# A planned encoder block on one core: paired reciprocals, a narrower port model, one more kind of wait, and new due times

## The chip, the cores and the metric

The kernel runs on one core of one Trainium2 chip. That core has a matrix engine (TensorE; PE in the profile, its weight loads PEld), a vector engine (VectorE; DVE), a scalar engine (ScalarE; ACT), a general engine (GpSimd; POOL) and a sync engine (SyncE; SP) that here only issues DMAs. Each engine takes its instructions in order; between engines, semaphores order them. The metric is the time of one execution on the device in microseconds (us); less is better. Three runs of the kernel before took 702.26, 703.32 and 703.99 us, median 703.32.

## What is computed

One encoder layer on 512 tokens of 1024 features, float32. In short (shapes, masks and gains left out where they don't matter here):

```python
hn = rms_norm(h, ln_mix)
z = hn @ w_in                      # 3590 columns, for three groups of heads
# A: 4 heads, two softmaxes each:  a = probs(q1, k1) - lam * probs(q2, k2);  o = a @ v; rms_norm(o)
# B: 6 heads, one softmax, bias from the cumulative log forget gate, causal
# C: 6 heads, one softmax, bias from a table of clipped relative positions
h = h + concat(o_a, o_b, o_c) @ w_out
u = rms_norm(h, ln_ffn) @ w_up     # 2 x 2816 columns
c = causal depthwise convolution of width 3 over u
h = h + (silu(gate) * val) @ w_down
h = h + (p @ w_ple_proj) * sigmoid(rms_norm(h, ln_ple) @ w_ple_gate)
```

Every query and key head is RMS-normed over its 64 features before the products. A softmax is `exp(s - max)` divided by its row sum; the division is a reciprocal of one number per row, and a multiplication of the row by it. For A, `probs(q1, k1)` and `probs(q2, k2)` have a reciprocal each, and the second is multiplied by `-lam` as well.

## The kernel before

**Products.** Matrices are float32, split into a high part of a shorter type (fp32r) and the rest: `split` casts a weight tile (`wraw`) to `whi` on ScalarE and subtracts on VectorE or GpSimd to get `wlo`. `mm3` then makes three products (high with high, high with low, low with high) into one bank of PSUM. There are eight banks, under the tags `z` (2), `s` (2), `t` (3) and `o` (1).

**Two stages, two plans.** The first stage (projections, attention, the output projection) and the second (the MLP, its down projection, the gate with the per-layer embedding) are each recorded as a list of operations before anything is issued. An object of class `Plan` then puts the list in order. All instructions are issued by one helper (`Engine.now`), so nearly all rows of the profile have line L363, and tiles tell them apart.

**How a plan makes an order.** `price` gives each operation a duration (`busy`) and a lag from its form and width. `due` gives each TensorE operation a due time: the sum of TensorE durations before it, plus a shift by the name of its group from the table `SHIFT`; every other operation is due ahead of the operations that need it. `solve` steps through time, and gives each engine that is free the ready operation that is due first, with a few rules for waiting a moment for a more urgent one. The order that comes out is the program order of all engines, and of the DMAs on SP's and POOL's queues. `SHIFT` has some 330 numbers between -30 and 30 us, of which no formula is given.

**The port in the plan.** `price` sets `op.port` for every GpSimd operation that is no DMA, and for VectorE's `tensor_scalar`, `tensor_tensor` and `scalar_tensor_tensor` whose inputs all lie outside PSUM. In `solve`, an operation with `port` of one of the two engines isn't begun while one of the other is under way. This is a matter of the plan; on the chip nothing enforces it but the order itself. There is one exception, in `emit`: in the second plan (where `late` is 0.1; in the first it is 0) a GpSimd operation of over `LONG` = 0.6 us by its price, whose predecessor among the operations with `port` is a VectorE operation, gets a true wait on that operation (`behind`).

**Attention.** `scores(pr, hh, qbs)` runs over blocks of 128 queries (`qb` 0 to 3) of head `hh` of a pair `pr`; the block `qb` has (qb + 1) x 128 keys. `softmax_map` makes the scores (two products into `s`), a combined add-bias and row minimum on VectorE into `e` and `st`, the exponential on ScalarE with its row sum into `st[:, 1:2]`, and the reciprocal on VectorE into `st[:, 2:3]`. Then GpSimd multiplies `e` by it (group B and C), or, for A, multiplies the second map's `e2` by its reciprocal and `-lam`, and VectorE joins both maps. `prob_cols` transposes the `e` of all four blocks of a head, and `values` makes the products with V into the bank `o`; the result goes to `oall` over `otmp`. `subln` norms the heads of A.

**The narrow GpSimd work.** `qk_sums` makes the norms of queries and keys: a square on ScalarE, a sum on VectorE, then for each token block a multiply and a power on GpSimd, 128x4 (`rs`); `qk_scale` on VectorE uses it to evacuate the bank into `zn`. `token_stats` does the like with one column (`rstd`). Between them GpSimd has the wide work: moves of halves of `q` and `k` (64x512), the scaling of `e`, some of the `wlo` subtractions of the first stage (`lo_by` chooses which, 128x768 and 128x512), sums and differences of weights in the second, and DMAs that add into a weight tile.

The price of the two kinds of GpSimd operation that matter for the wait: a subtraction of n columns is 0.1 + 0.0024 n us, a power of four columns 0.42 + 4 x 0.155, both times 1.05.

Of the kernel before, what the change touches and what calls it, by code (L numbers as in the profile page):

```python
# [8 lines left out]
F32 = mybir.dt.float32  # L9
# [3 lines left out]
ALU = mybir.AluOpType  # L13
# [28 lines left out]
for _i in range(3):  # L42
# [2105 lines left out]
```

## Time and profile before

| | us |
|---|---|
| median of three runs | 703.32 |
| the profiled execution | 702.13 |
| its span (first to last instruction) | 700.4 |
| TensorE busy | 686.6 |
| VectorE busy | 574.8 |
| ScalarE busy | 425.9 |
| GpSimd busy | 315.2 |

The span lies within the time of the execution. The granted TensorE clock is 1.0 for all of it. Busy times of different engines lie beside each other and don't add up to the span; a TensorE that is busy nearly all the time leaves other engines' idle time without a price of its own.

A row of the timeline has the start and the length in us, the engine, the line, the operation, what it writes and reads, its shapes and, in brackets, how long the engine was idle before it and what ended that. A row of waits has the engine and tile that waited, what it waited for, then us in total, how many times, and the longest.

### The profile page before, as it was taken

To read this page: it belongs to the slowest core of one execution; us is meant where nothing else is said; L and a number is where in the kernel's file an instruction comes from. 1 tells how busy PE (TensorE), PEld (TensorE's weight loads), DVE (VectorE), ACT (ScalarE), POOL (GpSimd) and SP (SyncE) were. 2 spreads that over 40 slices of the span, in tenths; PEclk is the share of its full clock that TensorE was granted. 3 is DMA by queue.
4 is the path that set the end of the run, shared out by engine and by line. 5 is a ranking of instruction groups with operands and counts; after the bars stand their busy time and mean duration, and the time that the engine had idled before them with its cause. 6 is when DMAs were issued, how large, how long until landed. Compare 5 with 4: busy or idle time off the path is not lost.

```text
span 700.4 us, 12856 instructions
## 1 busy us (share of the span) xinstructions
PE 686.6 (98%) x4600; PEld 642.4 (92%) x4600; DVE 574.8 (82%) x1159; ACT 425.9 (61%) x810; POOL 315.2 (45%) x418
## 2 busy tenths in 40 slices
PE   7999999999999999999999999999999999999997
PEld 7989999998899888899899899888999888999997
DVE  6788888888778766898989987889888889867777
ACT  6756776666557664766667644557445665436853
POOL 3686776757657544242332243232442312343650
PEclk9999999999999999999999999999999999999999
DMA  9533624333221152595875246774368663223433
GB/s 324 217 99 91 171 58 134 92 95 101 76 76 47 60 121 86 186 270 127 209 180 163 84 140 156 175 193 129 89 153 225 171 168 107 86 73 88 143 102 122
DMA packets 42989, 94.32 MB, mean 135 GB/s; under 512 B 4870, under 2 KB 9606, under 8 KB 42924
## 3 DMA queue, kind: packets, MB, share of 16 engines
q1 hardware_dynamic: 35868, 79.02, 35.8%
q0 software_dynamic: 6768, 14.16, 11.9%
q8 instruction: 36, 0.59, 0.3%
q10 hardware_dynamic: 288, 0.30, 0.1%
q14 instruction: 29, 0.24, 0.1%
HBM read 85.20 MB, written 4.21 MB: 128 GB/s over the span
## 4 chain that ended last, share of the span: by engine, by line
PE 89%; POOL 3%; DMA 3%; DVE 2%; issue 1%; ACT 1%; POOLq 0%; ACTq 0%; DVEq 0%
PE z L363 41%; PE s L363 21%; PE t L363 19%; PE o L363 8%; DMA wraw<-in_w_up_dram 2%; POOL k L363 2%; POOL q L363 1%; DMA zn<-in_w_in_dram 0%; POOL wraw L363 0%; DVE conv L363 0%; POOL wlo_again L363 0%; ACT whi L363 0%; DVE wlo L363 0%; ACT otmp L363 0%; DVE xl_again L363 0%
## 5 line engine op out<-in xcount | busy, mean ns | idle before, releaser
L363 ACT CAST whi<-wraw 128x768 fp32r<-128x768 f32 (+2 forms) x146 | 109.4, 762 | 51.9 <-PE z L363 16.5
L363 DVE TENSOR_TENSOR wlo<-wraw,whi 128x768 fp32r<-128x768 f32 (+2 forms) x128 | 113.8, 901 | 17.3 <-ACT whi L363 16.3
L363 PE MATMUL z<-whi,Th 128*128 128x384 f32 (+2 forms) x360 | 123.1, 348 | 4.6 <-ACT whi L363 4.6
L363 PE MATMUL z<-whi,Tl 128*128 128x384 f32 (+2 forms) x360 | 122.9, 347 | 0.1
L363 PE MATMUL z<-wlo,Th 128*128 128x384 f32 (+2 forms) x360 | 122.5, 346 | 0.0
L363 PEld LDWEIGHTS z<-whi,Th 128*128 128x128 f32 x360 | 67.9, 189 | 7.9 <-ACT whi L363 4.6
L363 PEld LDWEIGHTS z<-whi,Tl 128*128 128x128 f32 x360 | 67.8, 189 | 3.8 <-DVE Tl L363 0.5
L363 PEld LDWEIGHTS z<-wlo,Th 128*128 128x128 f32 x360 | 67.8, 189 | 3.2
L363 POOL TENSOR_TENSOR wraw<-wraw,wraw 128x768 f32<-128x768 f32 (+2 forms) x21 | 29.7, 1416 | 66.9 <-DVE pin L363 25.9
L363 ACT ACTIVATE e<-e,st 128x128 f32<-128x128 f32 (+3 forms) x80 | 44.7, 560 | 23.7 <-DVE st L363 23.0
L363 PE MATMUL s<-Tl,whi 128*128 128x512 f32 (+1 forms) x152 | 51.9, 341 | 0.0
L363 PE MATMUL s<-Th,whi 128*128 128x256 f32 (+1 forms) x152 | 51.7, 342 | 0.0
L363 PE MATMUL s<-Th,wlo 128*128 128x256 f32 (+1 forms) x152 | 51.7, 341 | 0.0
L363 PE MATMUL z<-Th,wlo 128*128 128x256 f32 (+1 forms) x152 | 51.4, 340 | 0.0
L363 PE MATMUL z<-Tl,whi 128*128 128x256 f32 (+1 forms) x152 | 51.3, 340 | 0.0
L363 PE MATMUL z<-Th,whi 128*128 128x256 f32 (+1 forms) x152 | 51.2, 341 | 0.0
L363 POOL TENSOR_TENSOR rs<-rs,nhalf 128x4 f32<-128x4 f32 x40 | 42.3, 1060 | 5.4 <-DVE rs L363 2.9
L363 DVE CUSTOM_DVE_ANT_0 e<-s,bias 128x128 f32<-128x128 f32 (+3 forms) x74 | 34.0, 471 | 11.7 <-PE s L363 9.1
L363 POOL TENSOR_SCALAR e<-e,st 128x512 f32<-128x512 f32 (+3 forms) x48 | 28.4, 602 | 24.4 <-DVE st L363 19.4
L363 PE MATMUL t<-wlo,ah 128*128 128x256 f32 x116 | 32.7, 282 | 0.0
L363 PE MATMUL t<-whi,al 128*128 128x256 f32 x116 | 32.7, 282 | 0.0
L363 PE MATMUL t<-whi,ah 128*128 128x256 f32 x116 | 32.4, 282 | 0.0
(341 smaller groups left out, 2281.2 us busy)
## 6 DMA issues: line engine op xcount, KB each, us to landing
wraw<-in_w_up_dram SPq DMA_DIRECT2D x41, 384.0 KB, 4.6
wraw<-in_w_in_dram SPq DMA_DIRECT2D x28, 384.0 KB, 3.9
wraw<-in_w_down_dram SPq DMA_DIRECT2D x17, 384.0 KB, 3.1
wlo_again<-in_w_up_dram SPq DMA_DIRECT2D x12, 384.0 KB, 3.7
whi_again<-in_w_up_dram SPq DMA_DIRECT2D x11, 384.0 KB, 3.9
wraw<-in_w_out_dram SPq DMA_DIRECT2D x16, 256.0 KB, 2.8
wraw<-in_w_up_dram SPq DMA_DIRECT2D x16, 256.0 KB, 4.1
wlo<-wraw POOLq DMA_DIRECT2D x7, 384.0 KB, 4.5
```

The source lines that it names most:

```text
L363: ins = getattr(self.eng, op)(*a, **k)
```

## The change

Four things are changed.

1. `softmax_map` no longer takes the reciprocal. `scores` gives two maps one tile `st` of 2 x 4 columns (six of them in turn, where there were twelve of 4), and takes both reciprocals in one VectorE instruction once both maps have their row sums. For A the two maps are those of one block; for B and C they are those of the blocks 0 and 1, and 2 and 3, and both scalings on GpSimd come after the second one's exponential.
2. In `price`, only an operation with an operand of at least 64 columns has `port`. So `rs`, `rstd` and other small GpSimd operations, and small VectorE ones, no longer hold the port or wait for it in the plan.
3. In `emit`, the wait of a GpSimd operation for the VectorE operation with `port` ahead of it is made in the first plan too, for operations of over 1.2 us by their price.
4. All numbers of `SHIFT` are new.

```diff
 SHIFT = {
-    "in1_1": 0.6, "in1_2": -16.6, "A0a": 11.4, "in1_3": 2.9, "in2_0": 13.5, "in2_1": 16, "A0b": 24, "in2_2": 0.5,
...
+    "in1_1": -30, "in1_2": -25.3, "A0a": -24.2, "in1_3": -30, "in2_0": -16, "in2_1": -7.6, "A0b": 0.1, "in2_2": 0.8,
...
 }
...
         here = [v for v in op.ins if v.tensor.space != bass.MemoryType.PSUM]
-        op.port = e == "pool" and not op.move or e == "dve" and (
-            len(here) == len(op.ins) and (op.name == "tensor_scalar" or op.name in ("tensor_tensor", "scalar_tensor_tensor")))
+        wide = max(self.width(v) for v in op.outs + op.ins) >= 64
+        op.port = wide and (e == "pool" and not op.move or e == "dve" and (
+            len(here) == len(op.ins) and op.name in ("tensor_scalar", "tensor_tensor", "scalar_tensor_tensor")))
...
             if op.port:
-                if before and op.eng.name == "pool" and before.eng.name == "dve" and op.busy > self.LONG and self.late:
+                if before and op.eng.name == "pool" and before.eng.name == "dve" and op.busy > (self.LONG if self.late else 1.2):
                     op.eng.behind(op.ins, before.ins)
                 before = op
...
-    def softmax_map(m, hh, qb, bias, rowb, name):
+    def softmax_map(m, hh, qb, bias, rowb, st, name):
...
-        st = ap.tile([P, 4], F32, tag="st", bufs=12, name=f"{name}_st")
...
         act.activation(e, e, AF.Exp, scale=-1.0, bias=init, accum_out=st[:, 1:2])
-        dve.reciprocal(st[:, 2:3], st[:, 1:2])
-        return e, st
+        return e
...
-        for qb in qbs:
+        maps = 2 if kind == "A" else 1
+        for n, qb in enumerate(qbs):
             bq = BIAS[pr, hh](qb)
             rowb = fq[:, qb, hd : hd + 1] if kind == "B" else None
-            e, st = softmax_map(QK[pr, 0], hh, qb, bq, rowb, f"{pr}_{hh}_{qb}")
-            if kind == "A":
-                yield
-                e2, st2 = softmax_map(QK[pr, 1], hh, qb, bq, rowb, f"{pr}_{hh}_{qb}b")
-                pool.tensor_scalar(e2, e2, st2[:, 2:3], X["nlam"], ALU.mult, ALU.mult)
-                dve.scalar_tensor_tensor(e, e, st[:, 2:3], e2, ALU.mult, ALU.add)
-            else:
-                pool.tensor_scalar(e, e, st[:, 2:3], 1.0, ALU.mult, ALU.mult)
-            PROB[pr, hh].append(e)
+            if maps == 2 or n % 2 == 0:
+                st = ap.tile([P, 2, 4], F32, tag="st", bufs=6, name=f"{pr}_{hh}_{qb}_st")
+                es = []
+            for m in range(maps):
+                es.append(softmax_map(QK[pr, m], hh, qb, bq, rowb, st[:, len(es)], f"{pr}_{hh}_{qb}_{m}"))
+                if m + 1 < maps:
+                    yield
+            if len(es) == 2:
+                dve.reciprocal(st[:, :, 2], st[:, :, 1])
+                e, e2 = es
+                if maps == 2:
+                    pool.tensor_scalar(e2, e2, st[:, 1, 2:3], X["nlam"], ALU.mult, ALU.mult)
+                    dve.scalar_tensor_tensor(e, e, st[:, 0, 2:3], e2, ALU.mult, ALU.add)
+                    es = [e]
+                else:
+                    for j in range(2):
+                        pool.tensor_scalar(es[j], es[j], st[:, j, 2:3], 1.0, ALU.mult, ALU.mult)
+                PROB[pr, hh] += es
```

87 rows, old and new, of the table SHIFT are left out of this document.

## The prediction, made before the result was known

> **What bounds the kernel now.** I read the head of the page first, then a table of two stretches, then who makes TensorE's weight loads wait, then the timeline around the longest waits.
>
> ```profile
> span 700.4 us, 12856 instructions
> ...
> PE 686.6 (98%) x4600; PEld 642.4 (92%) x4600; DVE 574.8 (82%) x1159; ACT 425.9 (61%) x810; POOL 315.2 (45%) x418
> ...
> PE 89%; POOL 3%; DMA 3%; DVE 2%; issue 1%; ACT 1%; POOLq 0%; ACTq 0%; DVEq 0%
> ```
>
> TensorE is busy 686.6 us of a span of 700.4, and the chain that ended last runs through it for 89%. What can be won is its idle time, so the next view splits that by the two plans of the kernel. Columns: stretch, length, then busy time and count for PE, PEld, DVE, ACT and POOL, the granted clock, DMA share, GB/s.
>
> ```profile
> 4.60:297.00 292.40, 288.04 (x1729) 268.27 (x1730) 231.68 (x646) 191.27 (x443) 177.58 (x275) 1.00 0.40 119
> 297.00:695.90 398.90, 398.50 (x2872) 374.09 (x2871) 340.77 (x508) 232.35 (x365) 133.98 (x133) 1.00 0.54 146
> ```
>
> The clock is 1.00 in both. The first plan (attention; its end at about 297 us is my reading) has 292.40 - 288.04 = 4.36 us of TensorE idle after the first product, the second (the MLP and the gate) 398.90 - 398.50 = 0.40. Before the first product and after the last lies what no order of the middle can win:
>
> ```profile
> 4.60 1.01 PE L363 MATMUL z<-whi,Th 128*128 128x384 f32 x2 [4.60 <-ACT whi L363]
> ```
>
> ```profile
> 695.65 0.28 PE L363 MATMUL z<-whi,al 128*128 128x256 f32 x1
> ...
> 697.39 0.33 SPq L363 DMA_DIRECT2D out_dram<-xl_again  x1
> ```
>
> The start costs 4.60 us (a load and a cast come first); from the last matmul to the end of the span run 700.4 - 695.65 = 4.75. Busy time on TensorE hides part of a stall, because a matmul's end lies well behind the start of the next one. The weight loads show the stalls from the other side (engine, tile, what it waited for: us, times, longest):
>
> ```profile
> PEld s L363 <- POOL k L363: 3.6, 4, 1.3
> PEld s L363 <- DVE st L363: 1.6, 3, 0.7
> PEld o L363 <- ACT otmp L363: 1.3, 1, 1.3
> PEld z L363 <- issue: 1.0, 4, 0.2
> PEld z L363 <- DVE conv L363: 0.9, 2, 0.6
> ```
>
> Without "issue", which waits for nothing that an order could change, the four named groups are 3.6 + 1.6 + 1.3 + 0.9 = 7.4 us. The two readings, 4.36 + 0.40 = 4.76 and 7.4, bound what is to be won from both sides; I take the middle, 6.1, that is 0.82 of each weight-load figure. So the whole change plays for under 0.9% of 703.3 us, and nothing in it makes a matmul shorter.
>
> **Where the waits come from.** The wait on `otmp` has its cause five us earlier:
>
> ```profile
> 156.79 1.87 POOL L363 TENSOR_TENSOR wlo<-wraw,whi 128x768 fp32r<-128x768 f32 x1 [0.23 <-ACT whi L363]
> ...
> 156.86 2.61 DVE L363 TENSOR_TENSOR wlo<-wraw,whi 128x768 fp32r<-128x768 f32 x1
> ```
>
> ```profile
> 160.56 0.69 DVE L363 TENSOR_TENSOR oall<-o,otmp 64x512 f32<-64x512 f32 x1
> ...
> 160.81 1.04 POOL L363 TENSOR_TENSOR rs<-rs,nhalf 128x4 f32<-128x4 f32 x1
> ...
> 161.29 0.63 ACT L363 ACTIVATE otmp<-oall 128x512 f32<-128x512 f32 x1 [1.30 <-DVE oall L363]
> 161.36 0.94 DVE L363 TENSOR_TENSOR wlo<-wraw,whi 128x768 fp32r<-128x768 f32 x1
> ...
> 161.97 0.30 PEld L363 LDWEIGHTS o<-otmp,oall 128*128 128x128 f32 x2 [1.26 <-ACT otmp L363]
> ```
>
> A long POOL subtraction starts 0.07 us ahead of a VectorE subtraction with two SBUF inputs, and the latter takes 2.61 us; the same form takes 0.94 us in the second fence. VectorE is late by 2.61 - 0.94 = 1.67 us, `oall` comes late, then `otmp`, and TensorE's load waits 1.26. The second fence shows a thing more: the `wlo` of 161.36 starts while a narrow POOL power (160.81, 1.04 us) is under way and isn't held up at all. The waits on `k` are the opposite collision:
>
> ```profile
> 176.23 0.95 DVE L363 TENSOR_TENSOR wlo<-wraw,whi 128x768 fp32r<-128x768 f32 x1
> 176.23 1.42 POOL L363 TENSOR_SCALAR k<-k 64x512 fp32r<-64x512 f32 x1
> ...
> 177.70 0.30 PEld L363 LDWEIGHTS s<-k,q 128*128 128x128 f32 x2 [1.33 <-POOL k L363]
> ```
>
> Both start at 176.23, VectorE goes first, and the POOL copy takes 1.42 us. All copies of that kind:
>
> ```profile
> L363 POOL TENSOR_SCALAR k<-k x30: 613/618/2027, 38.9 to 258.2; 64x512 fp32r<-64x512 f32 x30
> ```
>
> **The change, part by part.**
>
> *Reciprocals two at a time.*
>
> ```profile
> L363 DVE RECIPROCAL st<-st x80: 140/158/167, 43.9 to 268.0; 128x1 f32<-128x1 f32 x80
> ...
> L363 DVE SCALAR_TENSOR_TENSOR st<-st,fq x24: 200/214/683, 127.7 to 193.4; 128x1 f32<-128x1 f32 x24
> ```
>
> 40 of the 80 go: 40 x 0.158 = 6.3 us less on VectorE in the first plan (a two-element one costs what a one-element one does, since fixed cost is nearly all of 0.158 us; bounds for the saving 0 to 6.3). VectorE is busy 231.68 of 292.40 us there, so it has slack, and TensorE's weight loads wait for `st` only 1.6 us in all. I cost it through that term below. For the groups B and C the pair costs something: the first block's scaling waits for the second block's exponential, and then stands ahead of the second's on POOL.
>
> ```profile
> L363 POOL TENSOR_TENSOR rs<-rs,nhalf 128x4 f32<-128x4 f32 x40 | 42.3, 1060 | 5.4 <-DVE rs L363 2.9 <-DVE fa L363 0.2
> L363 POOL TENSOR_SCALAR k<-k 64x512 fp32r<-64x512 f32 x30 | 23.7, 792 | 5.6 <-ACT e L363 2.2 <-ACT k L363 2.1
> ...
> L363 POOL TENSOR_SCALAR rs<-rs,rstd 128x4 f32<-128x4 f32 x32 | 11.8, 368 | 22.9 <-DVE rs L363 21.5
> ...
> L363 POOL TENSOR_SCALAR e<-e,st 128x384 f32<-128x384 f32 x12 | 7.9, 664 | 1.6 <-DVE st L363 1.3 <-PE z L363 0.2
> ...
> L363 POOL TENSOR_TENSOR wlo<-wraw,whi 128x768 fp32r<-128x768 f32 x3 | 5.6, 1854 | 0.6 <-ACT whi L363 0.5
> ...
> L363 POOL TENSOR_TENSOR wlo<-wraw,whi 128x512 fp32r<-128x512 f32 x3 | 3.8, 1286 | 4.8 <-ACT whi L363 4.8
> ```
>
> (Columns: out<-in, shapes, count, busy us and mean ns, idle before.) The last pair of a head pays one 384-wide scaling, 0.664 us, between the last exponential and the last scaling. It is hidden by the projections that TensorE has queued beside the attention: in the list of its waits above no group on `e` reaches the 0.9 us of the last one shown. I take 0. Uncovered in all 12 heads it would be 12 x 0.664 = 8.0 us; I give that no more than the tail beyond the range. The four heads of A lose nothing, as their two maps were already joined at the second scaling.
>
> *Long POOL operations wait in the first plan too.* The rows above show which are over 1.2 us there: three subtractions of 768 (1.854 us) and three of 512 (1.286 us); the powers, at 1.060, and the copies of `k`, at 0.792, stay below. At most six waits are added. Behind a waiting one stand on POOL the next `rs`, `k` or `e`, late by at most one VectorE subtraction (0.94 us). What goes is the case of 156.8: I take the whole of its TensorE wait, 0.82 x 1.3 = -1.1 us (bounds 0 and -1.3).
>
> *Narrow operations no longer hold the port in the plan.* No instruction changes by this; the planner's clock does. Half of it fits the trace, by the `wlo` at 161.36: VectorE was planned around powers (40 of 1.060 us) that don't hold it. The other half does not:
>
> ```profile
> 106.16 0.68 DVE L363 SCALAR_TENSOR_TENSOR fbias<-otmp,fbias 128x512 f32<-128x512 f32 x1
> ...
> 106.34 1.42 POOL L363 TENSOR_SCALAR rs<-rs,rstd 128x4 f32<-128x4 f32 x1
> ...
> 106.75 0.95 DVE L363 TENSOR_TENSOR wlo<-wraw,whi 128x768 fp32r<-128x768 f32 x1
> ```
>
> A four-element POOL multiply, 0.262 us at its least, takes 1.42 us here and ends after two VectorE operations with two SBUF inputs. The new plan believes that it needn't wait. The Trainium skill, SBUF — State Buffer, section "Who interferes with whom", says that a VectorE instruction with two SBUF inputs contends with any GpSimd instruction that reads SBUF, and names no width; by that rule the narrow exemption would be wrong both ways. The trace agrees for POOL (1.42 us) and disagrees for VectorE (0.94 us beside a power). Going by the page alone, VectorE would gain nothing either, and the 2.2 us that I take below for `k` and `st` would be missing: about 703.2. What this does to the time is the second rival below.
>
> ```profile
> L363 POOL TENSOR_TENSOR rs<-rs,nhalf x40: 1006/1018/1487, 28.6 to 225.4; 128x4 f32<-128x4 f32 x40
> ...
> L363 POOL TENSOR_SCALAR rs<-rs,rstd x32: 262/267/1421, 44.2 to 224.9; 128x4 f32<-128x4 f32 x32
> ```
>
> Of the 32 multiplies more than half run at 0.267 or less; their excess is 11.8 - 32 x 0.262 = 3.4 us, and that of the powers 42.3 - 40 x 1.006 = 2.1. If a plan that no longer heeds them adds a third to these 5.5 us, POOL is 1.8 us later in all. How much of that TensorE feels I take from the `k` copies: 30 x (0.792 - 0.613) = 5.4 us of excess stand beside 3.6 x 0.82 = 3.0 us lost, 0.55. So +1.0 us (bounds: -0.6 if a third of the excess goes instead, +3.0 if it doubles). The narrow VectorE sum `st<-st,fq` (0.214 us, 0.683 at most) loses its place in the same way; its 24 cases are in that bound.
>
> *Due times chosen anew.* Every engine's order is drawn afresh, both plans, the loads on SP's queue and the POOL-issued ones among them. The `k` and `st` waits are missed appointments of an order that was meant to have none; a new order keeps some and makes others. Between 0 and all of them gone (bounds -0.82 x 5.2 = -4.3 and, if as many come as there were, +4.3) I take half of what there is, because VectorE's planned times now lie nearer to the measured ones: `k` -0.82 x 3.6 / 2 = -1.5, `st` -0.82 x 1.6 / 2 = -0.7. For the second plan I take 0, as it loses only 0.40 us.
>
> **Sum:** -1.1 + 1.0 - 1.5 - 0.7 = -2.3 us, to be held against the profiled execution: 702.13 us, its span of 700.4 and 1.7 around it, so a span of 698.1 and 699.8 us. The three runs shown have a median of 703.32, 1.2 above the profiled one; against it the forecast is **701.0 us**.
>
> **The rivals.**
>
> 1. *The waits move, and don't shrink:* half of the old ones go and as many come. For it: every order is new, and the collisions of `k` with `wlo` are between wide operations, which both plans treat alike. Against it: the measured case of 156.8. Time 703.3.
> 2. *Slower: narrow POOL work comes late.* The `rs` chain frees the projections' banks and opens the transposes. If its excess doubles, +5.5 x 0.55 = +3.0, and no other wait goes: 706.3. It decides from 2.1 / 0.55 = 3.8 us of added POOL excess on. For it: the 1.42 us row. Against it: `rs` is in none of the waits of TensorE shown, so a bank's slack takes some first.
> 3. *Slower: a load in the second plan comes too late for its split.*
>
> ```profile
> wraw<-in_w_up_dram SPq DMA_DIRECT2D x41, 384.0 KB, 4.6
> ```
>
> One such load exposed whole is 4.6 us; on top of rival 1 that gives 707.9. Against it: 0.40 us of idle in 398.90 means loads run well ahead.
> 4. *It doesn't do what it says:* the added wait is made only where a VectorE operation on the port stands directly ahead in the plan. If none of the six is so placed, and the collision comes again, 1.1 us of the sum are missing: 702.1.
>
> **How the numbers follow.** 0.3% of 703.3 is 2.1 us, about what a measurement of this kernel tells from no change, so faster means under 701.2 and slower over 705.4. Forecast 0.48 (own range 697.2, which is all 6.1 us won, to 701.2); rival 1 0.25; rival 4 0.10; rival 2 0.12; rival 3 0.05. Faster 0.48, same 0.25 + 0.10 = 0.35, slower 0.17. For the range I leave about 0.08 out below and 0.10 above: 697.5 lies just inside the ceiling, 706.5 just beyond rival 2 and short of rival 3.
>
> **What would show it.** Right: 40 reciprocals of two elements; no VectorE subtraction of 768 near 2.6 us in the first 297 us; weight-load waits for `k` near 1.8 us and for `otmp` gone; idle of TensorE after the first product near 2.5 us in the first plan and still under 1 in the second. The mean of the narrow `rs` multiplies should rise a little above 0.368 us. Wrong: new groups of waits of over 1 us on `rs`, `zn` or `e` (the pairing or the narrow ones cost what I hid), or loads and splits ahead of TensorE in the second plan; a start or an end that differs by more than 0.5 us would be a part that I held fixed.

## The result, and the profile after

The changed kernel takes 697.02 us (median of four runs, 696.18 to 697.96) against 703.41 for the kernel before (four runs): ratio 0.9912, 95% interval 0.9894 to 0.9929. That is 6.4 us less, where 2.3 were forecast, and 0.5 us below the low end of the range. The profiled execution took 696.18 us, 5.95 less than the profiled one of before.

The head of the page after, with the chain of waits (shares of the span by engine):

```profile
span 694.4 us, 12836 instructions
...
PE 684.5 (99%) x4600; PEld 642.3 (92%) x4600; DVE 570.7 (82%) x1119; ACT 424.9 (61%) x810; POOL 311.3 (45%) x418
...
PE 97%; POOL 1%; DMA 0%; DVE 0%; ACT 0%; issue 0%; POOLq 0%; ACTq 0%
```

The same two stretches as before, the second now up to the last matmul; the columns are stretch, length, then busy time and count for PE, PEld, DVE, ACT and POOL, clock, DMA share, GB/s:

```profile
4.60:297.00 292.40, 291.57 (x1753) 272.29 (x1754) 230.82 (x611) 193.99 (x450) 174.88 (x278) 1.00 0.42 123
297.00:689.90 392.90, 392.90 (x2848) 369.99 (x2846) 337.51 (x502) 228.64 (x358) 132.78 (x131) 1.00 0.54 145
```

TensorE's idle time after the first product falls from 4.36 to 292.40 - 291.57 = 0.83 us in the first stretch and from 0.40 to nothing in the second. Busy time hides part of a stall, so the matmuls themselves say more. By 297 us 1753 of them have begun, 24 more than before. Just before the end of the first stage there is a point where both kernels have made the same 1713 products, by tiles and shapes. The next matmul stands here first for the changed kernel and then for the one before; the third row is the last matmul of the changed kernel:

```profile
288.67 0.39 PE L365 MATMUL z<-whi,Th 128*128 128x512 f32 x1
```

```profile
293.83 0.39 PE L363 MATMUL z<-wlo,ah 128*128 128x512 f32 x1
```

```profile
689.67 0.28 PE L365 MATMUL z<-whi,al 128*128 128x256 f32 x1
```

At the first point the changed kernel is 293.83 - 288.67 = 5.2 us ahead. The last matmul starts 695.65 - 689.67 = 5.98 us earlier, so about 5 us are won in the first stage and about 1 us in the second; 694.4 - 689.67 = 4.7 us remain behind it, as before. The start is unchanged too. The whole gain lies in waits between, and the weight loads name them (engine, tile, what they waited for: us, times, longest):

```profile
PEld z L365 <- ACT whi L365: 4.6, 1, 4.6
PEld s L365 <- POOL k L365: 1.2, 4, 0.5
PEld z L365 <- ACT sq L365: 1.0, 1, 1.0
PEld t L365 <- DVE ptl L365: 0.4, 1, 0.4
```

The first row is the start. `k` has gone from 3.6 to 1.2 us. The six rows that are left out make 1.5 us, of 0.4 and less each; VectorE's `st` (1.6 before) and `conv` (0.9) and ScalarE's `otmp` (1.3) are in none of them. GpSimd's groups (out<-in, shapes, count, busy us and mean ns, idle before) and the new reciprocal:

```profile
L365 POOL TENSOR_TENSOR rs<-rs,nhalf 128x4 f32<-128x4 f32 x40 | 42.6, 1068 | 5.7 <-DVE rs L365 3.2
L365 POOL TENSOR_SCALAR k<-k 64x512 fp32r<-64x512 f32 x30 | 18.9, 630 | 1.9 <-ACT k L365 0.4
L365 POOL TENSOR_SCALAR rs<-rs,rstd 128x4 f32<-128x4 f32 x32 | 13.7, 427 | 18.9 <-DVE rs L365 16.4 <-DVE st L365 0.5 <-DVE V L365 0.4
...
L365 DVE RECIPROCAL st<-st 128x2 f32<-128x2 f32 x40 | 6.5, 162 | 2.6 <-ACT e L365 2.5
```

The wide copies of `k` hardly meet VectorE's wide work any more: seven of them took over 0.9 us before and one does now (0.93 us at 201.18), and their mean falls from 792 to 630 ns, near their undisturbed 613. The narrow `rs` multiplies go the other way, from 368 to 427 ns. The timeline (start, length, engine, operation; in brackets the idle time before and what ended it) has the one place where TensorE feels that:

```profile
222.34 0.69 DVE L365 TENSOR_TENSOR Tl<-oall,Th 128x512 fp32r<-128x512 f32 x1
...
222.40 1.50 POOL L365 TENSOR_TENSOR rs<-rs,nhalf 128x4 f32<-128x4 f32 x1
...
223.93 0.48 DVE L365 SCALAR_TENSOR_TENSOR zn<-z,rstd,rs 128x256 f32<-128x256 f32 x1 [0.91 <-POOL rs L365]
...
224.56 0.47 PE L365 MATMUL z<-whi,Th 128*128 128x512 f32 x1 [0.66 <-DVE zn L365]
```

A power, 1.006 us at its least before, takes 1.50 beside a VectorE operation with two SBUF inputs; `zn` waits 0.91 us for it and TensorE 0.66 for `zn`. The multiply just ahead, at 221.49, took 0.82 us in place of 0.262. The 1.0 us on `sq` among the weight loads is this same stall.

### The profile page after: what moved, and what is told of

The parts are those of the page before. It is cut to its first block, busy times and chain, and to the rows that moved or that the text cites. A ratio compares the mean times of both kernels' runs of the same rounds, so it can differ in the third digit from the quotient of the medians.

```text
span 694.4 us, 12836 instructions
## 1 busy us (share of the span) xinstructions
PE 684.5 (99%) x4600; PEld 642.3 (92%) x4600; DVE 570.7 (82%) x1119; ACT 424.9 (61%) x810; POOL 311.3 (45%) x418
## 3 DMA queue, kind: packets, MB, share of 16 engines
q0 software_dynamic: 6768, 14.16, 11.8%
## 4 chain that ended last, share of the span: by engine, by line
PE 97%; POOL 1%; DMA 0%; DVE 0%; ACT 0%; issue 0%; POOLq 0%; ACTq 0%
PE z L365 46%; PE s L365 23%; PE t L365 20%; PE o L365 8%; POOL rs L365 1%; DMA zn<-in_w_in_dram 0%; POOL q L365 0%; POOL k L365 0%; DVE zn L365 0%; DVE xl_again L365 0%; ACT q L365 0%; ACT whi L365 0%; ACT xl_again L365 0%; DVE ptl L365 0%; DVE rs L365 0%
## 5 line engine op out<-in xcount | busy, mean ns | idle before, releaser
L365 PE MATMUL s<-Th,whi 128*128 128x512 f32 (+1 forms) x152 | 51.3, 341 | 0.0
L365 PE MATMUL z<-Th,wlo 128*128 128x512 f32 (+1 forms) x152 | 51.2, 341 | 0.0
L365 POOL TENSOR_TENSOR rs<-rs,nhalf 128x4 f32<-128x4 f32 x40 | 42.6, 1068 | 5.7 <-DVE rs L365 3.2
L365 POOL DMA_DIRECT2D wraw<-in_w_up_dram x21 | 18.3, 883 | 38.4 <-DMA wraw<-in_w_up_dram 26.1
L365 POOL TENSOR_SCALAR e<-e,st 128x256 f32<-128x256 f32 (+3 forms) x48 | 26.6, 566 | 17.2 <-DVE st L365 16.6
```

What stands on the lines that cost most here:

```text
L365: ins = getattr(self.eng, op)(*a, **k)
```

## The experiments

Each ratio is against the kernel before on the same chip (medians of 702.2 to 703.1 us), with its 95% interval; times in us of different groups of runs come from different chips, so the ratios compare better. "Idle" is TensorE's idle time between 4.6 and 297 us.

### One part at a time, with the order held

These four keep every engine's order, as orders come from the plan and the edits are made at the issue of an instruction. First the changed kernel without the added wait:

```diff
-                if before and op.eng.name == "pool" and before.eng.name == "dve" and op.busy > (self.LONG if self.late else 1.2):
+                if before and op.eng.name == "pool" and before.eng.name == "dve" and op.busy > self.LONG and self.late:
```

> The changed kernel in the same order on every engine, without the three waits that the first plan's rule adds (two subtractions of 128x768 on POOL, one of 128x512). If the wait carries the gain (my step: -1.1 us): the POOL subtraction and a VectorE one with two SBUF inputs collide again, VectorE is late by up to 1.7 us, and the time goes from 697.0 to about 698. If the new order carries it: 697.0, within 0.5.

Measured: 698.59 us, ratio 0.9942 (0.9925 to 0.9958). The timelines of the place, in the changed kernel and then without the wait:

```profile
180.97 0.96 DVE L365 TENSOR_TENSOR wlo<-wraw,whi 128x768 fp32r<-128x768 f32 x1
...
182.16 1.84 POOL L365 TENSOR_TENSOR wlo<-wraw,whi 128x768 fp32r<-128x768 f32 x1 [1.22 <-PE t L365]
```

```profile
180.59 1.84 POOL L365 TENSOR_TENSOR wlo<-wraw,whi 128x768 fp32r<-128x768 f32 x1
180.66 2.58 DVE L365 TENSOR_TENSOR wlo<-wraw,whi 128x768 fp32r<-128x768 f32 x1
...
184.03 0.33 PE L365 MATMUL t<-ident,zn 128*128 128x128 f32 x1 [0.92 <-DVE ptl L365]
```

The collision of before comes back (2.58 us in place of 0.96), and TensorE stands 0.92 us. Idle goes from 0.83 to 1.76. As the order is the same, each matmul can be held against its own: 0.97 us are lost at this place and 1.2 us near 356 us, in the second stage, where nothing was changed. There a load comes late. The same GpSimd sum there, in the changed kernel and then without the wait:

```profile
352.26 0.74 POOL L365 TENSOR_TENSOR wraw<-wraw 128x256 f32<-128x256 f32 x1 [2.32 <-DVE wlo L365]
```

```profile
354.69 0.74 POOL L365 TENSOR_TENSOR wraw<-wraw 128x256 f32<-128x256 f32 x1 [3.52 <-DMA wraw<-in_w_up_dram]
```

It waits for VectorE in the one and for a DMA in the other. The load before that one, also issued by GpSimd, took 9.45 us to land in place of 8.25; GpSimd waited for it, and issued the next at 349.19 us in place of 347.83. The next two runs of the changed order have this late load and a stall behind it near 356 us too, whatever their edit, so it isn't laid to the wait. In all three the first stage ends 0.8 to 1.5 us later than in the changed kernel; whether the load is late because of that stays open. Of the changed kernel one execution has a trace, its fastest of four.

Second, the changed kernel with 80 reciprocals of one element in the places of the 40:

```diff
+            if op.name == "reciprocal" and len(op.a[0].ap) > 1 and op.a[0].ap[1][1] == 2:
+                for j in range(2):
+                    op.ins = op.eng.now(op.name, [real(v)[:, j : j + 1] for v in op.a], {})
+                continue
```

> The changed kernel in the same order, but each two-element reciprocal is issued as two of one element, one behind the other: 80 again, 40 x 0.16 = 6.3 us more on VectorE in the first plan. If VectorE's load there is what TensorE waited for: 1 to 3 us slower than 697.0. If it is slack (my reading was that it counts only by the waits on st): under 0.7 us.

Measured: 697.99 us, ratio 0.9939 (0.9922 to 0.9955), idle 292.40 - 291.47 = 0.93 us. That is 1.0 us over the changed kernel's 697.02, and more by the ratios, so by the time alone it is no case of slack. The trace puts most of the loss elsewhere. VectorE is busy 232.65 us in the first stretch, only 1.8 more, and TensorE's idle is 0.1 us longer. Matmul by matmul the run is 0.24 us late at 8.6 us, ahead of the first reciprocal (58.3 us), and 0.76 at 182 us. The other 2.4 us of its 3.2 arise near 356 and 453 us, where the first stage's reciprocals are long past. Fewer reciprocals as such bring at most 0.5 us.

Third, both undone at once, so that only the new order remains:

> The changed kernel with its order on every engine, but with the reciprocals one at a time and without the added waits, so that only the new order is left of the change. Theory A (the order carries the gain; the wait is worth 1.1 to 1.6 us as in the run without it, the pairing nothing): 698.3 to 699.5 us, ratio 0.994 to 0.997 (0.9942 was measured without the waits), TensorE idle of 1.5 to 2.5 us between 4.6 and 297 us. Theory C (the pairing and the wait help only together, and undoing both costs more than the sum): 700.5 us or more.

Measured: 698.76 us against 702.63, ratio 0.9943 (0.9928 to 0.9958), idle 1.85. The order alone is worth 0.57% (0.42 to 0.72), 4.0 us of the 6.2 that 0.9912 makes. Matmul by matmul against the changed kernel, 1.1 us are lost at the place of the wait and 1.65 near 356 us, of 3.2 in all. So the order may be worth more than 4.0 us, if the late load isn't its own.

Fourth, the reverse: the kernel before with nothing but the wait, so the first diff the other way round. Three of its six long subtractions get it.

> The kernel before with its order on every engine and one edit, the added wait of GpSimd operations of over 1.2 us in the first plan; three of six subtractions get it. Theory A (the collision at 156.8 us goes, as the prediction's step had it): 1.1 us less than the kernel before, ratio 0.9984, no VectorE subtraction of 768 columns near 2.6 us there, and no wait on otmp. Rival 4 of the prediction (the wait is not on the VectorE operation that collides): no change, ratio 1.000, the subtraction stays at 2.6 us.

Measured: 702.37 us against 702.63, ratio 1.0002 (0.9985 to 1.0019). That holds the 1.000 of rival 4, and theory A's 0.9984 lies just outside. The trace decides what the times can't:

```profile
157.95 0.95 DVE L363 TENSOR_TENSOR wlo<-wraw,whi 128x768 fp32r<-128x768 f32 x1
...
159.04 1.85 POOL L363 TENSOR_TENSOR wlo<-wraw,whi 128x768 fp32r<-128x768 f32 x1 [1.39 <-ACT ptc L363]
```

```profile
4.60:297.00 292.40, 288.98 (x1730) 269.40 (x1731) 230.31 (x646) 191.37 (x444) 177.85 (x275) 1.00 0.40 119
```

The subtraction that took 2.61 us takes 0.95, GpSimd's now stands behind it, `otmp` holds up no load, and idle falls from 4.36 to 3.42. Matmul by matmul this run is 1.04 us late at 10.1 us, ahead of anything that the edit touches, and level again at the load of `otmp` (161.94 us against 161.97), so about 1.1 us are won at that place. The mechanism is as predicted; that the time of an execution falls by it isn't shown.

### Due times exchanged, and taken away

The changed kernel with the table of before, and the kernel before with the new table:

```diff
 SHIFT = {
-    "in1_1": -30, "in1_2": -25.3, "A0a": -24.2, "in1_3": -30, "in2_0": -16, "in2_1": -7.6, "A0b": 0.1, "in2_2": 0.8,
+    "in1_1": 0.6, "in1_2": -16.6, "A0a": 11.4, "in1_3": 2.9, "in2_0": 13.5, "in2_1": 16, "A0b": 24, "in2_2": 0.5,
...
```

> The changed kernel with the due times of before: paired reciprocals, the new port rule and the added wait, in an order of their own. Theory A (the plan's clock now fits the chip, whatever the due times): most of the gain stays, about 698 to 699.5. Theory B (the gain lies in due times chosen for this plan): 702 to 706, with stalls of TensorE of 6 to 12 us after the first product.

> The kernel before with the new due times alone. Theory A: about as before, 702 to 704, since the plan still misjudges narrow operations. Theory B: the due times fit another plan, so 703 or more, up to 710. A third theory, that the due times are better by themselves: under 699.

Measured: 735.21 us, ratio 1.0464 (1.0445 to 1.0483), and 732.44 us, 1.0421 (1.0396 to 1.0445). Idle is 18.0 and 19.4 us, and both times lie far above what either theory gave. The granted clock, 1.00 in the two kernels, falls to 0.95 and 0.93 in single stretches of 50 us, so part of the loss should be slower matmuls. These two tables are worth something only with the plan for which they were made; under the other rule each is worse than none, as the next four show. They have no table at all (`SHIFT = {}`): the changed kernel; the kernel before; the changed kernel with the old port rule (`wide = True`); and the changed kernel with one reciprocal for each map, taken at once and used as before. All but the kernel before have the added wait.

```diff
         act.activation(e, e, AF.Exp, scale=-1.0, bias=init, accum_out=st[:, 1:2])
+        dve.reciprocal(st[:, 2:3], st[:, 1:2])
         return e
...
-            if len(es) == 2:
-                dve.reciprocal(st[:, :, 2], st[:, :, 1])
+            if maps == 2:
```

> The changed kernel with an empty table of shifts, so that every due time is the plain sum of TensorE's work before it. Theory A (the three parts of the change make a plan that the chip can keep, and due times only polish it): 700 to 710, far under the 735 of due times that were chosen for another plan. Theory B (all lies in the choice of due times): 725 to 740, like the two runs with borrowed due times.

> The kernel before with an empty table of shifts. Theory A: at least 6 us slower than the changed kernel with an empty table, most of it in the first 300 us. Theory B: the same as that one within 3 us.

> The changed kernel with an empty table and the port rule of before, in which narrow operations hold the port in the plan; paired reciprocals and the added wait stay. If the port rule is the part that counts: within 3 us of the kernel before with an empty table. If pairing and wait count: within 3 us of the changed kernel with an empty table.

> The changed kernel with an empty table and one reciprocal for each map, taken and used as before; the new port rule and the added wait stay. If the port rule is the part that counts: within 2 us of the changed kernel with an empty table. If the pairing counts: slower by 3 to 8 us, about VectorE's 40 x 0.16 = 6.4 us.

| without a table | us | ratio (95%) | idle, us |
|---|---|---|---|
| old rule, single (before) | 719.71 | 1.0245 (1.0219 to 1.0271) | 7.61 |
| old rule, paired | 715.64 | 1.0209 (1.0154 to 1.0263) | 5.87 |
| new rule, paired (after) | 712.20 | 1.0150 (1.0099 to 1.0202) | 5.48 |
| new rule, single | 708.22 | 1.0078 (1.0057 to 1.0099) | 1.56 |

The new rule, with the wait, takes 11.5 us off the single kernel; that is clear of noise. The steps between neighbours in the table are not, as their intervals overlap or touch: the new rule takes 3.4 us off the paired kernel, and pairing takes 4.1 off under the old rule (with the wait) and adds 4.0 under the new one. With the order held, pairing was worth at most 0.5 us; so such 4 us, if they are real, are those of another order, which any edit to the list may draw. The changed kernel without a table is 2 us above the 710 of theory A and far under theory B; the kernel before is 7.5 us slower still, as theory A had it. Of the last two runs neither came out as one of its two expectations had it, least of all the single kernel, which is 4 us faster where 3 to 8 slower or no change was expected.

### Due times searched for each rule

If a table belongs to its plan, each rule should be judged with tables of its own. For each kernel here a table was searched by random changes, kept where the plan ended earlier by its own prices, somewhat varied; no time of the chip went into it. Two tables were made for three of the rules, the second with a somewhat shorter search. How far each search went isn't shown here. The third rule is the one that the rows above suggest for narrow operations: they wait in the plan for a wide one of the other engine, but hold up none.

```diff
-        wide = max(self.width(v) for v in op.outs + op.ins) >= 64
-        op.port = wide and (e == "pool" and not op.move or e == "dve" and (
+        op.wide = max(self.width(v) for v in op.outs + op.ins) >= 64
+        op.port = (e == "pool" and not op.move or e == "dve" and (
...
-            if op.port:
+            if op.port and op.wide:
                 held[e] = t0 + busy
```

> The changed kernel with one edit, the port rule of before (narrow operations hold the port in the plan), and due times searched for this plan. The three kernels sent with it got a search of the same length. It answers whether the gain belongs to the port rule or to a lucky table. Theory A (the port rule: with narrow operations on the port some waits of TensorE on k, st or oall can't be planned away): 700 to 704 us, TensorE idle of 2 to 5 us between 4.6 and 297 us, copies of k with a mean of 0.70 us or more. Theory B (the luck of a table; any rule does as well when its due times are searched): within 1.5 us of the kernel with due times searched under the new rule, idle under 1.5 us.

> The changed kernel without the pairing (a reciprocal for each map, each map scaled at once), with the new port rule and the new wait, and due times searched for this plan. Theory A (the port rule and due times made for it carry the gain, pairing nothing): 696 to 699 us, idle of TensorE under 1.5 us between 4.6 and 297 us. Theory C (pairing is needed, since it takes 6 us off VectorE): 700 us or more, with waits on st or zn of over 1 us.

> The changed kernel with all its code, and a table of due times searched afresh in the same way as for the other kernels sent here. It is the control: it tells how far two tables made for one plan differ. Theory A: 696 to 699 us, idle of TensorE under 1.5 us between 4.6 and 297 us, as in the changed kernel. Theory B (the changed kernel's table is a lucky one): 700 us or more.

> The changed kernel with the port rule that the traces show: a narrow GpSimd operation waits in the plan for a wide VectorE one with two SBUF inputs, but holds up none itself; due times searched for this plan. Theory A with this asymmetry: narrow rs multiplies fall back from a mean of 0.427 us to 0.35 us or less, the one wait on rs at 222 us goes, 695.5 to 697.5 us. If the narrow delay costs TensorE nothing anyway (it was felt once, for 0.7 us): within 1 us of the kernel with due times searched under the new rule, with the shorter rs multiplies all the same.

The old rule came out as its theory A had it in time and idle (702.52 us, 2.14 us), though its `k` copies did not (0.674 us). The single kernel, at 703.18 us, is where theory C had it, with loads waiting 2.5 us on `st`; but pairing isn't what it lacks, since the paired control came out worst, 707.14 us. That is ten above the changed kernel with the same code, as theory B had it: the changed kernel's table is a lucky one, or a better searched one. The third rule's 698.08 us lies 0.6 above its expectation, and not by the way given: its `rs` multiplies average 0.455 us, not under 0.35, and one wait on `rs` (1.0 us) remains. In the control's trace stands why it is slow, in part:

```profile
130.16 2.15 POOL L363 TENSOR_TENSOR wlo<-wraw,whi 128x768 fp32r<-128x768 f32 x1
130.21 0.08 DVE L363 DVE_READ_ACCUMULATOR2_ANT st<- 128x1 f32 x1
130.33 2.01 DVE L363 SCALAR_TENSOR_TENSOR st<-st,fq 128x1 f32<-128x1 f32 x1
...
132.99 0.50 PE L363 MATMUL s<-k,q 128*128 128x512 f32 x1 [1.21 <-DVE st L363]
```

The narrow sum `st<-st,fq`, 128 x 1 with two SBUF inputs, takes 2.01 us beside a wide GpSimd subtraction, where 0.21 is usual. The new rule says that it needs no port. What follows it on VectorE is late, and TensorE stands 1.21 us for it. The next run tests this: the same order, with three subtractions issued behind the sums that they met, and made to wait for them.

```diff
+        for p in [q for q in order if q.port and q.eng.name == "pool" and q.busy > 1.2 and not self.late]:
+            met = [q for q in order if q.narrow and p.start - q.busy < q.start < p.start + p.busy]
...
+                    order.insert(order.index(met[-1]) + 1, p)
...
+                op.eng.behind(op.ins, last[id(op)].ins)
```

> The run with due times searched afresh (707.14 us), with the same order on every engine, but three GpSimd subtractions of 768 columns of the first plan wait for the narrow VectorE sum st<-st,fq that they met in it. In that run two of these sums took 2.01 and 1.38 us beside a subtraction, and TensorE stood 1.37 us at 131.4 right after the first. Theory D (the new rule forgets that a narrow VectorE operation is held up by a wide GpSimd one, and a table that lets them meet pays for it): the sums fall to 0.3 us or less there, the waits on st fall by 1.2 to 2.5 us, and the time to 704.5 to 706.0 us. Theory B (these meetings are hidden, or the waiting GpSimd work is late in its turn): 706.5 to 708 us.

Measured: 704.45 us, 2.7 less, ratio 1.0024 (1.0014 to 1.0033); the two traces lie 2.2 us apart.

```profile
130.43 0.22 DVE L373 SCALAR_TENSOR_TENSOR st<-st,fq 128x1 f32<-128x1 f32 x1
130.57 0.28 DVE L373 CUSTOM_DVE_ANT_0 e<-s,bias 128x128 f32<-128x128 f32 x1
130.74 1.84 POOL L373 TENSOR_TENSOR wlo<-wraw,whi 128x768 fp32r<-128x768 f32 x1 [0.20 <-DVE st L373]
```

The sum is back at 0.22 us, and the subtraction is only 0.6 us later. So the harm of the narrow VectorE exemption is shown, at 2 to 3 of the 10 us; TensorE's stalls that are left behind the start are of 1.1 us at most, and no run here takes them apart. Then a second table for each rule:

> The changed kernel with the port rule of before and a second table of due times, searched for that plan. Theory A (the rule sets what a table can reach): 700 to 705 us, near the first table's 702.5. Theory B (luck of the table): 5 us or more from the first table of the same rule, in either direction.

> The changed kernel with a second searched table. Theory D (the new rule leaves narrow VectorE sums to meet wide GpSimd work, so that tables for it scatter by what they happen to meet): anywhere from 697 to 708 us, with a mean of the 24 sums st<-st,fq that goes with the time (0.268 us in the changed kernel, 0.382 in the first searched table). Theory A (the new rule alone makes good tables, and the first searched one was a bad draw): 696 to 699 us.

> The rule by which narrow operations of both engines wait in the plan for wide ones but hold up none, with a second searched table. Theory D (this rule is the one that the chip follows, so its tables come out near each other): 697 to 700 us, the sums st<-st,fq at a mean under 0.3 us. Theory B (the first table's 698.1 was luck): 701 us or more.

| rule, table | us | ratio (95%) | idle, us | matmuls by 297 us | longest `st` sum, us |
|---|---|---|---|---|---|
| old, its own (before) | 703.41 | 1 | 4.36 | 1729 | 0.68 |
| old, paired, first | 702.52 | 0.9997 (0.9980 to 1.0015) | 2.14 | 1739 | 0.23 |
| old, paired, second | 702.43 | 1.0001 (0.9990 to 1.0012) | 4.06 | 1725 | 0.65 |
| new, its own (after) | 697.02 | 0.9912 (0.9894 to 0.9929) | 0.83 | 1753 | 0.68 |
| new, paired, first | 707.14 | 1.0069 (1.0055 to 1.0084) | 5.69 | 1709 | 2.01 |
| the same, behind the sums | 704.45 | 1.0024 (1.0014 to 1.0033) | 4.75 | 1720 | 0.58 |
| new, paired, second | 705.88 | 1.0054 (1.0036 to 1.0073) | 5.43 | 1718 | 1.74 |
| new, single | 703.18 | 1.0016 (1.0006 to 1.0027) | 4.48 | 1722 | 1.53 |
| third, paired, first | 698.08 | 0.9941 (0.9925 to 0.9957) | 1.14 | 1754 | 0.49 |
| third, paired, second | 701.09 | 0.9989 (0.9969 to 1.0010) | 1.52 | 1741 | 0.68 |

The last column is the longest of the 24 sums in each trace, from rows like these, of the changed kernel and of the first searched table of its rule (shortest, median and longest in ns, first and last start in us):

```profile
L365 DVE SCALAR_TENSOR_TENSOR st<-st,fq x24: 199/218/681, 117.0 to 175.7; 128x1 f32<-128x1 f32 x24
```

```profile
L363 DVE SCALAR_TENSOR_TENSOR st<-st,fq x24: 194/218/2008, 130.3 to 190.2; 128x1 f32<-128x1 f32 x24
```

All three searched tables of the new rule let a sum meet a wide subtraction (1.5 to 2.0 us), and all are slower than the kernel before. The kernel's own table lets one meet only the end of a subtraction (0.46 us at 153.31; its longest, 0.68, stands beside another wide GpSimd operation), and none of the tables under the other two rules lets a subtraction hold one up. The rule alone doesn't decide it: in the kernel before with the exchanged table a sum takes 1.88 us beside a subtraction, and in the single kernel without a table none takes over 0.60. So what was expected of tables under the new rule, 696 to 699 us, fell in all three. The second tables for the old and the new rule came out as theories A and D had them (with a mean sum of 0.371 us in the latter). The old rule's two tables agree within 0.1 us. The third rule's two are the fastest searched ones, but they lie 3 us apart, the second's interval overlaps the old rule's, and its 701.09 us is where theory B (the first was luck) had it; that this rule makes better tables is suggested, not shown. None beats the changed kernel.

## Why the prediction fell short

**The bound held, in part by luck.** TensorE's waits were put between 4.76 and 7.4 us, 6.1 in the middle; 5.98 went, and 4.6 us ahead and 4.7 behind stayed as they were. That nothing makes a matmul shorter held too. But 6.1 us weren't all that there was. With the smaller groups and "issue", which the prediction left out, weight loads waited 10.1 us behind the start before and wait 4.1 now, in groups of 0.2 us and more; "issue" alone fell from 1.5 to 0.4 with the new order.

**The step that failed is "Due times chosen anew": "a new order keeps some and makes others", so "I take half of what there is".** It gave -1.5 for `k`, -0.7 for `st` and 0 for the second plan. The new order keeps few: of 7.4 us of named waits of weight loads 1.2 are left on `k`, and the new ones in the rows shown are 1.0 on `sq` and 0.4 on `ptl`. The order alone, measured, brings 4.0 us; the prediction's terms that are matters of order, -1.5 - 0.7 + 1.0, made 1.2. The 0 for the second plan was wrong by about 1 us, and the prediction's own rows had it: the 0.9 us on `conv` that it counts into its 7.4 lie at 469.81 and 568.03 us, in the second plan, where busy time hid them from the 0.40 us of idle. The reason given for the half (VectorE's planned times now lie nearer to the measured ones) doesn't carry the result either: under the same rule other tables give 705.9 and 707.1 us. The term's bounds, 4.3 us either way, are narrower than the spread: the control lies 4.8 us above the kernel before, and the exchanged tables 30. How this table was found can't be read from the kernel, and why just it is so good stays open beyond the `st` sums.

**Narrow operations, +1.0.** The direction was right. The `rs` rows grew by 13.7 - 11.8 + 42.6 - 42.3 = 2.2 us, near the 1.8 taken. TensorE felt 0.66 us of that, once, so the share of 0.55 taken from the `k` copies was too high: it is 0.66 / 2.2 = 0.3. The other half of the step, the narrow VectorE sum, was put into the bound with its longest case of 0.68 us. It can take 2.01, and a table that lets it happen loses 2.7 us: that this is near rival 2's +3.0 is luck, as rival 2 meant another operation, and this kernel's table avoids it.

The Trainium skill, SBUF — State Buffer, section "Who interferes with whom", makes no exception for narrow operations. For the sum beside a wide subtraction the trace agrees (2.01 us against 0.21), as it does for the power at 222.40; for the wide subtraction beside a narrow power it didn't (0.94 us, in the prediction). The third rule is what these rows show, made into a plan.

**The wait, -1.1.** Right: 0.9 us of idle in both directions and 1.0 to 1.1 by the matmuls, and the collision comes and goes with it. Rival 4 was wrong in the trace: in the kernel before with the wait three of six subtractions wait, the one of 156.8 us among them.

**The pairing, 0.** Right within half a microsecond: there are 40 reciprocals at 0.162 us for two elements, and what they save is of hardly any use to TensorE. It is less than 6.3 us, too: VectorE's time in them falls from the 11.5 us of this row of before to 6.5.

```profile
L363 DVE RECIPROCAL st<-st 128x1 f32<-128x1 f32 x80 | 11.5, 157 | 4.6 <-ACT e L363 4.3
```

The cover of the later scaling held in this kernel, where no load waits for `e`. In the first searched table of the new rule one does:

```profile
PEld t L363 <- POOL e L363: 0.9, 1, 0.9
```

But the single kernel with its searched table, which has no pairing, has 1.4 us of the same wait, so it isn't laid to the pairing.

**Rivals 1 and 3.** Most waits didn't move but went, and loads of the second plan stayed ahead (idle 0.00 there). Rival 3 was near all the same: in the three edited runs of the same order a load did come late, for 1.2 to 1.65 us.

## What to carry to other kernels

Where a planner draws the order, an edit to its rules and the table tuned for them are one thing: exchange either alone and 30 us are lost here, and two tables for the same code differ by 10. So such a change is to be read in the trace, and its parts priced with the order held; a forecast has no ground to halve the remaining waits, and should give the draw a spread as wide as other tables for the same code show. A port rule for a plan should say for each pair who is held up: by the traces here narrow operations should wait for wide ones, and need not hold them up; that a plan is faster by this isn't shown.

## What the runs showed of the hardware that was not expected

A VectorE operation on one column takes 2.01 us, ten times its usual 0.21, when a 128x768 GpSimd subtraction of 2.15 us starts 0.17 us ahead of it: it ends with the subtraction, so its width is no protection. The other way round width counts: in the prediction's rows a 128x768 VectorE subtraction keeps its 0.94 us beside a four-column GpSimd power. In the changed kernel's trace five more begin under such a power that is under way (27.53, 31.31, 51.10, 75.18 and 150.44 us); they take 0.95 to 0.96 us and the powers their usual 1.01 to 1.02.
